# A mixture-of-experts kernel on one core: expert 0 computed in the small form too, so that small and large experts alternate from the start

## The chip, the core and the metric

The kernel runs on one core of a Trainium2 chip. The metric is device microseconds (us) of one execution; lower is better. A core has five instruction streams that run by themselves and meet at semaphores: TensorE (PE, matmuls; its weight loads are shown apart as PEld), VectorE (DVE), ScalarE (ACT), GpSimd (POOL) and SyncE (SP, which here issues nearly all DMAs). PE reads SBUF and writes PSUM, a small memory of eight banks. PE's clock has two levels, 1.2 and 2.4 GHz; the profile gives the granted share of the higher one.

## The reference, cut to what matters

Two layers over 256 tokens of width 1024. Each is a mixer (differential attention, pooling, a gated recurrence, one output projection), a layer norm, a feed-forward part and a layer norm. In layer 0 the feed-forward part is a dense SwiGLU; in layer 1 each token goes to the best 2 of 8 experts, and this is where the change lies:

```python
def _swiglu(x, w_gate, w_up, w_down):
    return (jax.nn.silu(x @ w_gate) * (x @ w_up)) @ w_down

def _moe_swiglu(x, w_router, w_gate, w_up, w_down):
    logits = (xt @ w_router).astype(jnp.float32)
    top_logit, top_e = lax.top_k(logits, TOP_K)          # 2 of 8
    gate = jax.nn.softmax(top_logit, axis=-1)
    ...                                                  # rows of each expert gathered
    ys = lax.map(expert_block, ...)                      # _swiglu(rows, w_gate[e], w_up[e], w_down[e])
    contrib = ys[dest] * gate.reshape(-1)[order][:, None]
    return jnp.zeros_like(xt).at[tok].add(contrib)
```

An expert's matrices are 1024 x 2816, 1024 x 2816 and 2816 x 1024 in float32, 34.6 MB together; all eight are read once, 276.8 MB of the 344.8 MB that the core reads from HBM.

## The kernel before

**Two forms of an expert.** A *large* expert has 128 places for tokens. Each 1 MB tile of its weights (`weight`, L102 to L117) is split into a high part (ACT, L112) and a rest (DVE, L114), and every product is three matmuls at one pass each: high x high, high x low, low x high (`up_part`, L941; `down_part`, L1014). Its stationary operands are the gathered tokens `xgh`, `xgl`, 128 columns wide. A *small* expert has 64 places. Its weights are used as they come, in float32, without a split (`small_up_part`, L960; `small_down_part`, L986): a matmul has 64 stationary columns (`xs`, `hs`), and two that stand side by side use the two column halves of the array. The profile shows each float32 matmul as two records.

**Which expert is which.** Position 0 of the order is always expert 0. The others are ranked by their number of tokens (`order_experts`, L900, on DVE: comparisons and sums over 8 x 8 tables), and `RANKS` says which rank stands at which position: 0, 5, 1, 6, 2, 7, 3, 4. Ranks 5 to 7 (the three with the fewest tokens) are small, the others, expert 0 among them, large. The numbers of the chosen experts are loaded into registers of SP (`weights_at`, L1091), which computes the weights' addresses from them.

**Groups.** `GROUPS` says which positions are gathered together (`gather`, L852): for each group, 32 matmuls pick the tokens' rows with a one-hot matrix `O` and leave them in PSUM; copies bring them to `xgh`, `xgl` (large) and `xs` (small). Before, groups are expert 0 alone, three times small with large, and the last large one alone.

**The step loop.** (L1100 and on) An expert is cut into chunks of its 2816 hidden columns: 512 (large) or 1024 (small). In each step the gate and up products of a chunk are issued, and the down products of the chunk before it. An expert's last chunk issues the next group's gather; an expert's result is spread back to the tokens by one-hot matmuls and added with the gate's factor (`combine`, `small_combine`). A scheduler orders each engine's instructions by a simulated timeline, within what dependences allow.

**Buffers.** Weight tiles go through a ring of 13 buffers of 1 MB (5 in `rawp`, 8 in `more`), used in turn. SP issues a tile's DMA when its buffer is free: in a large expert when ACT and DVE have split it, in a small one when PE has multiplied with it.

**Too many tokens.** `overflow` (L1149) runs a loop over all experts when any expert has more tokens than places. In the profiled execution it is skipped.

Of the kernel before, what the change touches and what calls it, by code (L numbers as in the profile page):

```python
# [8 lines left out]
F32 = mybir.dt.float32  # L9
F32R = mybir.dt.float32r  # L10
I32 = mybir.dt.int32
# [5 lines left out]
P = 128  # L17
T = 256
NT = T // P
D = 1024  # L20
KD = D // P
# [6 lines left out]
NE = 8  # L28
# [10 lines left out]
FILL = (6, 4, 5)  # L39


RANKS = (0, 5, 1, 6, 2, 7, 3, 4)
FIRST_SMALL = 5
SMALL = tuple(r >= FIRST_SMALL for r in RANKS)
GROUPS = ((0,), (1, 2), (3, 4), (5, 6), (7,))
HALF = 64
TINY, EDGE = 160, 480

# [7 lines left out]
def trunk(ctx, tc, x, w_in, w_out, col_params, row_params, block_params,  # L56
          ln1_g, ln1_b, ln2_g, ln2_b, ffn_w_gate, ffn_w_up, ffn_w_down,
          router_w, moe_w_gate, moe_w_up, moe_w_down, out):
    nc = tc.nc
    vec, act, gp, pe = nc.vector, nc.scalar, nc.gpsimd, nc.tensor  # L60
# [668 lines left out]
    place = R("place", [P, NT, NE])  # L729
# [84 lines left out]
    mo = moe.enter_context(tc.tile_pool(name="mo", bufs=1))  # L814
    acc = x_nat
    mot = moe.enter_context(tc.tile_pool(name="mot", bufs=1))
    M = lambda nm, shape, dt=F32, tag=None: (mo if tag else mot).tile(shape, dt, tag=tag or "m_" + nm, name="m_" + nm)
# [14 lines left out]
    def places(place_cols, small):  # L832

        O = const.tile([P, NT, 2, P], F32R, tag="O", name="O")
        for t in range(NT):
            for j, of_half in enumerate(small):
                last = vec.tensor_scalar(O[:, t, j, :], halves.rearrange("p a b -> p (a b)") if of_half else slots,
                                         place_cols[:, t, j:j + 1], None, op0=ALU.is_equal)
        return O[:, :, 0:len(small), :], last

    def turn_places(O):

        n = O.shape[2]
        OT = mo.tile([P, 2, NT, P], F32R, tag="OT", name="OT")
        tp = psC.tile([P, 2, NT, P], F32, tag="tp", name="tp")
        for j in range(n):
            for t in range(NT):
                pe.transpose(tp[:, j, t, :], O[:, t, j, :].bitcast(F32), ident)
        act.copy(OT[:, 0:n, :, :], tp[:, 0:n, :, :])
        return OT  # L850

    def gather(O, small, wide=False):  # L852

        n = len(small)
        xg = (mo.tile([P, KD, P], F32R, tag="xgh", name="xgh"), mo.tile([P, KD, P], F32R, tag="xgl", name="xgl"))
        xs = mo.tile([P, KD, HALF], F32, tag="xs", name="xs") if small[0] else None
        for k in range(0, KD, 2):
            for i in range(2):
                pool, tag = (psA, "gu") if wide else ((psD, "sg"), (psC, "tp"))[i]
                ps = pool.tile([P, 2, 2, P], F32, tag=tag, name="ps_g")  # L860
                for j in range(2):
                    for t in range(NT):
                        pe.matmul(ps[:, j, 0:n, :], xn[i][:, t, (k + j) * P:(k + j + 1) * P], O[:, t, :, :],
                                  start=(t == 0), stop=(t == NT - 1))
                (vec.tensor_copy if i and not wide else act.copy)(xg[i][:, k:k + 2, :], ps[:, :, n - 1, :])
                if xs is not None:
                    part_ = ps[:, :, 0, 0:HALF]
                    act.copy(xs[:, k:k + 2, :], part_) if i == 0 else vec.tensor_add(xs[:, k:k + 2, :], xs[:, k:k + 2, :], part_)
        return xg, xs
# [26 lines left out]
        vec.tensor_mul(gate, gate, den[:, :, None].to_broadcast([P, NT, NE]))  # L896

    small64 = M("small64", [P, NE])

    def order_experts():  # L900

        key = M("key", [P, NE])
        vec.tensor_copy(key, tokens)
        vec.memset(key[:, 0:1], float(2 * T))
        le = key[:, :, None].to_broadcast([P, NE, NE])
        lj = key[:, None, :].to_broadcast([P, NE, NE])
        c1 = M("c1", [P, NE, NE], tag="yh")
        c2 = M("c2", [P, NE, NE], tag="yl")
        rank = M("rank", [P, NE])
        vec.tensor_tensor(c1, lj, le, op=ALU.is_gt)  # L910
        vec.tensor_tensor(c2, lj, le, op=ALU.is_equal)
        vec.tensor_mul(c2, c2, lower)
        vec.tensor_add(c1, c1, c2)
        vec.reduce_sum(rank, c1, axis=AX.X)

        vec.tensor_tensor(c1, rank[:, None, :].to_broadcast([P, NE, NE]), ranks[:, :, None].to_broadcast([P, NE, NE]),
                          op=ALU.is_equal)
        at = M("at", [P, NE])
        vec.tensor_mul(c2, c1, numbers[:, None, :].to_broadcast([P, NE, NE]))
        vec.reduce_sum(at, c2, axis=AX.X)  # L920
        vec.tensor_copy(chosen, at)
        for src, name in ((place, "place_s"), (gate, "gate_s")):
            to = M(name, [P, NT, NE])
            for t in range(NT):
                vec.tensor_mul(c2, c1, src[:, t, None, :].to_broadcast([P, NE, NE]))
                vec.reduce_sum(to[:, t, :], c2, axis=AX.X)
            routed.append(to)

        vec.tensor_scalar(small64, rank, float(FIRST_SMALL), float(P - HALF), op0=ALU.is_ge, op1=ALU.mult)
        vec.tensor_add(at, tokens, small64)  # L930
        vec.tensor_reduce(key[:, 0:1], at, axis=AX.X, op=ALU.max)
        vec.tensor_copy(count, key[:, 0:1])

# [3 lines left out]
    def expert_weights(e):  # L937

        return [w[0][bass.ds(e, 1), :, :].rearrange("e a b -> (e a) b") for w in (moe_w_gate, moe_w_up, moe_w_down)]
# [57 lines left out]
    def glu(pg, pu, n):  # L997
        sg = mo.tile([P, FC], F32, tag="sg", name="sg")
        act.activation(sg[:, :n], pg[:, :n], AF.Silu)  # L999
        vec.tensor_mul(sg[:, :n], pu[:, :n], sg[:, :n])  # L1000
        return sg

    def turn(f, n, hh, last=False):

        nk = n // P
        tp = psC.tile([P, 4, P], F32, tag="tp", name="tp_h")
        for k in range(nk):
            pe.transpose(tp[:, k, :], hh[:, k * P:(k + 1) * P], ident)
        tags = ("xgh", "xgl") if last else ("hTh", "hTl")
        hT = [mo.tile([P, 2, 2, P], F32R, tag=tag, name="hT").rearrange("p a b c -> p (a b) c") for tag in tags]  # L1010
        split_to(hT[0][:, :nk, :], hT[1][:, :nk, :], tp[:, :nk, :])
        return hT

    def down_part(ws, py, f, n, hT):  # L1014

        nk = n // P
        for k0 in range(0, nk, 2):
            w = weight(rows(ws[2], f // P + k0, 2))
            for k in range(2):
                first, last = f + k0 + k == 0, f + (k0 + k + 1) * P == DFF  # L1020
                halves = [(py[nn], slice(nn * 512, (nn + 1) * 512)) for nn in range(2)]
                for i in range(2):
                    for ps, s in halves:
                        pe.matmul(ps, hT[i][:, k0 + k, :], w[k][0][:, s], start=(first and i == 0), stop=False)  # L1024
                for ps, s in halves:
                    pe.matmul(ps, hT[0][:, k0 + k, :], w[k][1][:, s], start=False, stop=last)  # L1026
# [14 lines left out]
    def y_banks():  # L1041
        return [psB.tile([P, 512], F32, tag="y", name="py") for n in range(2)]
# [103 lines left out]
                act.activation(acc[:, t, :], x_nat[:, t, :], AF.Copy, scale=ALPHA)  # L1146


    def overflow():  # L1149
        most = nc.values_load(count[0:1, 0:1], min_val=0, max_val=T + P - HALF)  # L1150
        with tc.If(most > P):
            rings[:] = [rawp] * RAW_BUFS
            hold[:] = [None]
            vec.tensor_add(place, place, small64[:, None, :].to_broadcast([P, NT, NE]))
            for _ in range(2):
                vec.tensor_scalar_add(slots, slots, float(P))
                with tc.For_i(0, NE, 1) as e:
                    pg_e = mot.tile([P, 2, NT, 2], F32, tag="pg_e", name="pg_e")
                    for j in range(2):
                        vec.tensor_copy(pg_e[:, 0, :, j:j + 1], place[:, :, bass.ds(e, 1)])  # L1160
                        vec.tensor_copy(pg_e[:, 1, :, j:j + 1], gate[:, :, bass.ds(e, 1)])
                    O, _ = places(pg_e[:, 0, :, :], (False,))
                    OT = turn_places(O)
                    xg, _ = gather(O, (False,))
                    ws = expert_weights(e)
                    py = y_banks()
                    for f, n in chunks:
                        down_part(ws, py, f, n, turn(f, n, glu(*up_part(ws, xg, f, n), n)))
                    combine(OT[:, 0, :, :], pg_e[:, 1, :, 0:1], py)
            for t in range(NT):  # L1170
                vec.reduce_sum(sums[:, t, :], acc[:, t, :].rearrange("p (a b) -> p a b", a=2), axis=AX.X)
            squares(sums)
# [45 lines left out]
```

## Time and profile before

| what | us |
|---|---|
| median of 3 runs (1137.21 to 1139.38) | 1137.24 |
| the profiled execution | 1140.82 |
| its span, first to last instruction | 1139.1 |
| PE busy in the span | 1100.1 |
| DVE busy in the span | 734.4 |
| ACT busy in the span | 590.7 |

The span is cut into pieces by the trace: up to about 414 us lie layer 0, the mixer of layer 1 and the routing, then the eight experts, and the last 17 us are the sums of the last expert, the layer norm and the output. PE's busy time has modelled ends, so a busy PE is not yet a PE at its peak. A row `x4` of a timeline stands for four instructions in a row.

### The profile page before, as it was taken

To read this page: it belongs to the slowest core of one execution; us is meant where nothing else is said; L and a number is where in the kernel's file an instruction comes from. 1 tells how busy PE (TensorE), PEld (TensorE's weight loads), DVE (VectorE), ACT (ScalarE), POOL (GpSimd) and SP (SyncE) were. 2 spreads that over 40 slices of the span, in tenths; PEclk is the share of its full clock that TensorE was granted. 3 is DMA by queue.
4 is the path that set the end of the run, shared out by engine and by line. 5 is a ranking of instruction groups with operands and counts; after the bars stand their busy time and mean duration, and the time that the engine had idled before them with its cause. 6 is when DMAs were issued, how large, how long until landed. Compare 5 with 4: busy or idle time off the path is not lost. (4 is left out here: it accounts for less than half of the span.)

```text
span 1139.1 us, 15821 instructions
## 1 busy us (share of the span) xinstructions
PE 1100.1 (97%) x6017; PEld 848.3 (74%) x6017; DVE 734.4 (64%) x938; ACT 590.7 (52%) x798; POOL 25.4 (2%) x64
## 2 busy tenths in 40 slices
PE   8989999999998999999999999999999999999995
PEld 8978999999897888874357883347883347888883
DVE  6777655455867669961148972048972049898986
ACT  5764544444466458750146751046751046777673
POOL 1001000000100100000000000000000000000000
PEclk9989999999998969999999999999999999999998
DMA  9732755565464849989999999999999999999931
GB/s 320 279 115 92 259 186 186 186 186 185 153 215 148 332 161 354 375 296 378 411 414 412 411 407 388 380 413 412 410 419 393 376 413 412 407 411 367 360 119 39
DMA packets 158660, 346.93 MB, mean 305 GB/s; under 512 B 8164, under 2 KB 59504, under 8 KB 158576
## 3 DMA queue, kind: packets, MB, share of 16 engines
q1 hardware_dynamic: 158400, 345.56, 81.1%
q8 instruction: 49, 0.80, 0.3%
q14 instruction: 35, 0.29, 0.1%
q10 hardware_dynamic: 144, 0.26, 0.1%
q0 software_dynamic: 32, 0.02, 0.0%
HBM read 344.77 MB, written 1.05 MB: 304 GB/s over the span
## 5 line engine op out<-in xcount | busy, mean ns | idle before, releaser
L114 DVE TENSOR_TENSOR lo<-raw,hi 128x1024 fp32r<-128x1024 f32 x446 | 525.4, 1219 | 151.8 <-ACT hi L112 149.2
L112 ACT CAST hi<-raw 128x1024 fp32r<-128x1024 f32 x446 | 444.6, 1050 | 139.8 <-issue 54.1
L144 PE MATMUL mm<-xh,hi 128*128 128x256 f32 x512 | 147.2, 288 | 0.0
L146 PE MATMUL mm<-xl,hi 128*128 128x256 f32 x512 | 146.2, 286 | 0.0
L145 PE MATMUL mm<-xh,lo 128*128 128x256 f32 x512 | 146.1, 286 | 0.0
L1024 PE MATMUL py<-hi,hT 128*128 128x512 f32 x432 | 117.4, 392 | 0.0
L144 PEld LDWEIGHTS mm<-xh,hi 128*128 128x128 f32 x512 | 99.6, 195 | 0.9
L145 PEld LDWEIGHTS mm<-xh,lo 128*128 128x128 f32 x512 | 99.5, 194 | 0.4
L146 PEld LDWEIGHTS mm<-xl,hi 128*128 128x128 f32 x512 | 99.4, 194 | 0.0
L1024 PEld LDWEIGHTS py<-hi,hT 128*128 128x128 f32 x432 | 80.3, 188 | 17.6 <-issue 0.8
L955 PE MATMUL pg<-hi,xgh 128*128 128x512 f32 (+1 forms) x240 | 90.3, 381 | 3.2 <-ACT hi L112 3.2
L955 PE MATMUL pg<-hi,xgl 128*128 128x512 f32 (+1 forms) x240 | 89.1, 376 | 0.0
L955 PE MATMUL pu<-hi,xgh 128*128 128x512 f32 (+1 forms) x240 | 88.4, 374 | 0.0
L955 PE MATMUL pu<-hi,xgl 128*128 128x512 f32 (+1 forms) x240 | 88.0, 372 | 0.0
L1000 DVE TENSOR_TENSOR sg<-pu,sg 128x512 f32<-128x512 f32 (+2 forms) x39 | 25.2, 645 | 88.1 <-PE pu L972 65.1
L957 PE MATMUL pg<-lo,xgh 128*128 128x512 f32 (+1 forms) x240 | 69.9, 379 | 0.5 <-DVE lo L114 0.4
L1026 PE MATMUL py<-lo,hT 128*128 128x512 f32 x216 | 69.0, 401 | 0.0
L972 PE MATMUL pg<-raw,xs 128*64 128x512 f32 (+1 forms) x288 | 68.9, 563 | 0.0
L972 PE MATMUL pu<-raw,xs 128*64 128x512 f32 (+1 forms) x288 | 68.8, 561 | 0.0
L957 PE MATMUL pu<-lo,xgh 128*128 128x512 f32 (+1 forms) x240 | 68.7, 374 | 0.0
L999 ACT ACTIVATE sg<-pg 128x512 f32<-128x512 f32 (+2 forms) x39 | 21.9, 561 | 88.5 <-PE pg L957 49.5
L994 PE MATMUL py<-raw,hs 128*64 128x512 f32 x264 | 60.4, 599 | 0.7 <-ACT hs L983 0.7
(296 smaller groups left out, 1416.5 us busy)
## 6 DMA issues: line engine op xcount, KB each, us to landing
raw<-in_moe_w_down_dram SPq DMA_DIRECT2D x87, 1024.0 KB, 10.5
raw<-in_moe_w_gate_dram SPq DMA_DIRECT2D x79, 1024.0 KB, 11.4
raw<-in_moe_w_up_dram SPq DMA_DIRECT2D x79, 1024.0 KB, 11.3
raw<-in_w_in_dram SPq DMA_DIRECT2D x17, 1024.0 KB, 5.6
raw<-in_ffn_w_gate_dram SPq DMA_DIRECT2D x11, 1024.0 KB, 5.2
raw<-in_ffn_w_up_dram SPq DMA_DIRECT2D x11, 1024.0 KB, 5.2
raw<-in_ffn_w_down_dram SPq DMA_DIRECT2D x11, 1024.0 KB, 5.0
raw<-in_moe_w_gate_dram SPq DMA_DIRECT2D x12, 768.0 KB, 7.6
```

Of the source, the lines that this page charges most:

```text
L112: act.copy(hi, raw[:, s, :])
L114: last_lo[:] = [vec.tensor_sub(lo, raw[:, s, :], hi.bitcast(F32))]
L144: pe.matmul(ps, lh, rh, start=first, stop=False)
L145: pe.matmul(ps, ll, rh, start=False, stop=False)
L146: return pe.matmul(ps, lh, rl, start=False, stop=last)
L955: pe.matmul(ps[:, :n], xg[i][:, k0 + k, :], w[k][0], start=(k0 + k + i == 0), stop=False)
L957: pe.matmul(ps[:, :n], xg[0][:, k0 + k, :], w[k][1], start=False, stop=(k0 + k == KD - 1))
L972: pe.matmul(ps[h * HALF:(h + 1) * HALF, :n], xs[:, k0 + k, :], raw[:, k, h * n:(h + 1) * n], start=(k0 + k == 0), stop=(k0 + k == KD - 1))
L994: pe.matmul(py[nn * HALF:(nn + 1) * HALF, :], hs[:, k % nk, k // nk, :], raw[:, k - k0, nn * 512:(nn + 1) * 512], start=(f + k == 0), stop ...
L1000: vec.tensor_mul(sg[:, :n], pu[:, :n], sg[:, :n])
L1024: pe.matmul(ps, hT[i][:, k0 + k, :], w[k][0][:, s], start=(first and i == 0), stop=False)
L1026: pe.matmul(ps, hT[0][:, k0 + k, :], w[k][1][:, s], start=False, stop=last)
```

## The change

Expert 0 gets the small form, with 64 places. The positions become expert 0 (small), rank 1 (large), rank 5 (small), rank 2 (large), rank 6 (small), rank 3 (large), rank 7 (small), rank 4 (large). Expert 0 and the large one behind it are gathered each by itself; the rest in pairs small with large. `gather` makes no large copies where the group has no large expert. `ends` keeps each expert's token number (with 64 added for the small ones), and the loop of `overflow` looks at each expert's before it does the work, which moved into `more_places`.

```diff
-RANKS = (0, 5, 1, 6, 2, 7, 3, 4)
+RANKS = (0, 1, 5, 2, 6, 3, 7, 4)
 FIRST_SMALL = 5
-SMALL = tuple(r >= FIRST_SMALL for r in RANKS)
-GROUPS = ((0,), (1, 2), (3, 4), (5, 6), (7,))
+SMALL = tuple(r == 0 or r >= FIRST_SMALL for r in RANKS)
+GROUPS = ((0,), (1,), (2, 3), (4, 5), (6, 7))
...
-        xg = (mo.tile([P, KD, P], F32R, tag="xgh", name="xgh"), mo.tile([P, KD, P], F32R, tag="xgl", name="xgl"))
+        xg = None if small[-1] else [mo.tile([P, KD, P], F32R, tag=tag, name="xg") for tag in ("xgh", "xgl")]
...
-                (vec.tensor_copy if i and not wide else act.copy)(xg[i][:, k:k + 2, :], ps[:, :, n - 1, :])
+                if xg is not None:
+                    (vec.tensor_copy if i and not wide else act.copy)(xg[i][:, k:k + 2, :], ps[:, :, n - 1, :])
...
+    ends = M("ends", [P, NE], I32)
...
+        vec.memset(small64[:, 0:1], float(P - HALF))
         vec.tensor_add(at, tokens, small64)
+        vec.tensor_copy(ends, at)
...
-            for _ in range(2):
+            for r in range(2):
                 vec.tensor_scalar_add(slots, slots, float(P))
                 with tc.For_i(0, NE, 1) as e:
...
+                    end = nc.values_load(ends[0:1, bass.ds(e, 1)], min_val=0, max_val=T + P - HALF)
+                    with tc.If(end > (r + 1) * P):
+                        more_places(e)
```

Lines behind the changed ones move by a few numbers: L955, L957 become L959, L961 (large up products), L972 becomes L976 (small up), L994 becomes L998 (small down), L969 and L991 (their DMAs) L973 and L995, L1094 becomes L1098.

PE at the start of the experts, before: behind the gather (`ps_g`) of expert 0 stand large matmuls, three for each piece of weight (`hi`, `lo`).

```order
L792 MATMUL pc<-r_sel,ones 128x8
L863 MATMUL ps_g<-O,xn 128x128 x32
L955 MATMUL pg<-hi,xgh 128x512
L955 MATMUL pg<-hi,xgl 128x512
L955 MATMUL pg<-hi,xgh 128x512
L955 MATMUL pg<-hi,xgl 128x512
L957 MATMUL pg<-lo,xgh 128x512 x2
```

The same place of the changed kernel: small matmuls on the unsplit weights (`raw`, `xs`), and the transposes of the first chunk's product (`tp_h`) behind 56 of them, 24 of these from the second chunk; then the down products (`py`), more up products, and the gather of the next expert in pieces of 8.

```order
L863 MATMUL ps_g<-O,xn 128x128 x32
L976 MATMUL pg<-raw,xs 64x512 x8
...
L985 MATMUL tp_h<-ident,sg 128x128 x4
L976 MATMUL pg<-raw,xs 64x512 x4
...
L998 MATMUL py<-raw,hs 64x512 x16
...
L863 MATMUL ps_g<-O,xn 128x128 x8
L998 MATMUL py<-raw,hs 64x512 x12
L863 MATMUL ps_g<-O,xn 128x128 x8
L998 MATMUL py<-raw,hs 64x512 x4
L959 MATMUL pg<-hi,xg 128x512 x4
```

So the first expert's large matmuls are gone from there, and large ones begin behind three chunks of small ones.

SP before, at the loads of the expert numbers into registers (`m_chosen`; `count` is the highest token number): they stand behind the 21st weight tile, with one more tile among them.

```order
L107 DMA raw<-in_moe_w_up_dram 128x4x512
L107 DMA raw<-in_moe_w_down_dram 128x2x1024
L1094 TENSOR_LOAD m_chosen
...
L107 DMA raw<-in_moe_w_down_dram 128x2x1024
L1094 TENSOR_LOAD m_chosen
...
L1150 TENSOR_LOAD count
L1150 ISA x2
L107 DMA raw<-in_moe_w_gate_dram 128x4x512
```

SP in the changed kernel: the eight loads (seven of `m_chosen`, one of `count`) stand together, behind the 13th weight tile and ahead of the 14th.

```order
L973 DMA raw<-in_moe_w_up_dram 128x2x1024
L973 DMA raw<-in_moe_w_gate_dram 128x2x1024
L1098 TENSOR_LOAD m_chosen
...
L1168 TENSOR_LOAD count
L1168 ISA x2
L973 DMA raw<-in_moe_w_up_dram 128x2x1024
L973 DMA raw<-in_moe_w_gate_dram 128x2x1024
```

The loads have moved ahead by eight tiles. On DVE the sums that they read from are no longer mixed with splits (L114) but follow each other, with the adds of the gather between.

## Rows read from the trace of the kernel before

**Rows 1.** The page: PE, and the bytes moved in 40 slices.
```profile
PE 1100.1 (97%) x6017; PEld 848.3 (74%) x6017; DVE 734.4 (64%) x938; ACT 590.7 (52%) x798; POOL 25.4 (2%) x64
GB/s 320 279 115 92 259 186 186 186 186 185 153 215 148 332 161 354 375 296 378 411 414 412 411 407 388 380 413 412 410 419 393 376 413 412 407 411 367 360 119 39
```
**Rows 2.** Windows, one for each stage: length, busy time (count), clock, DMA, GB/s.
```profile
core 0: us, PE busy (x) PEld busy (x) DVE busy (x) ACT busy (x) POOL busy (x), PEclk, DMA share, GB/s
414.20:508.70 94.50, 94.50 (x448) 79.00 (x447) 81.74 (x104) 70.52 (x78) 0.00 (x0) 0.97 0.93 342
508.70:679.70 171.00, 169.17 (x788) 105.20 (x787) 94.17 (x102) 75.69 (x96) 0.00 (x0) 1.00 1.01 398
679.70:851.00 171.30, 166.29 (x786) 103.75 (x785) 96.45 (x104) 77.04 (x96) 0.00 (x0) 1.00 1.02 402
851.00:1022.30 171.30, 166.10 (x788) 103.93 (x787) 96.86 (x102) 79.45 (x97) 0.00 (x0) 1.00 1.03 402
1022.30:1122.10 99.80, 99.80 (x482) 83.54 (x481) 88.68 (x89) 71.09 (x84) 0.00 (x0) 1.00 0.69 254
```
**Rows 3.** Timeline of PE at four places: start, us, what.
```profile
414.21 0.73 PE L955 MATMUL pg<-hi,xgh 128*128 128x512 f32 x1
...
821.42 0.39 PE L955 MATMUL pg<-hi,xgh 128*128 128x512 f32 x1
...
1090.93 0.39 PE L955 MATMUL pg<-hi,xgh 128*128 128x512 f32 x1
...
1121.69 0.39 PE L146 MATMUL py<-lo,hT 128*128 128x512 f32 x1
```
**Rows 4.** Waits of PE in 679.7 to 851: total us, times, longest.
```profile
PE tp_h L981 <- DVE sg L1000: 2.5, 3, 0.9
PE pg L955 <- ACT hi L112: 1.6, 1, 1.6
PE ps_c L1074 <- ACT yh L130: 0.7, 1, 0.7
PE ps_c L1074 <- DVE yl L130: 0.2, 1, 0.2
```
**Rows 5.** Windows at the start of the experts.
```profile
414.00:416.00 2.00, 2.00 (x6) 1.64 (x7) 0.00 (x0) 0.37 (x1) 0.00 (x0) 0.50 1.00 403
416.00:418.00 2.00, 2.00 (x6) 1.58 (x5) 0.66 (x1) 1.04 (x1) 0.00 (x0) 0.50 1.04 395
418.00:420.00 2.00, 2.00 (x7) 1.58 (x7) 0.75 (x4) 1.05 (x1) 0.00 (x0) 0.67 0.36 141
```
**Rows 6.** Timeline of PE: combine, small up products, gather, down products.
```profile
705.35 0.50 PE L1060 MATMUL ps_c<-yh,OT 128*128 128x512 f32 x1
...
706.02 1.94 PE L972 MATMUL pg<-raw,xs 128*64 128x512 f32 x8
...
848.62 1.11 PE L863 MATMUL ps_g<-O,xn 128*128 128x256 f32 x8
849.57 0.63 PE L1026 MATMUL py<-lo,hT 128*128 128x512 f32 x2
850.04 1.08 PE L1024 MATMUL py<-hi,hT 128*128 128x512 f32 x4
```
**Rows 7.** Timeline of SP: the 13th weight tile, and the issues around the register loads.
```profile
383.54 1.24 SPq L107 DMA_DIRECT2D raw<-in_moe_w_gate_dram  x1
...
434.03 2.96 SPq L107 DMA_DIRECT2D raw<-in_moe_w_down_dram  x2
439.95 0.37 SPq L107 DMA_DIRECT2D raw<-in_moe_w_gate_dram  x1
```
**Rows 8.** Timeline of DVE: token sums, the first splits, the highest count.
```profile
407.53 0.17 DVE L794 COPY r_tokens<-pc 128x8 f32<-128x8 f32 x1 [0.26 <-PE pc L792]
...
407.89 5.79 DVE L114 TENSOR_TENSOR lo<-raw,hi 128x1024 fp32r<-128x1024 f32 x5
...
438.55 0.14 DVE L932 CAST count<-m_key 128x1 int32<-128x1 f32 x1
```
**Rows 9.** Windows: mostly a large expert, and a small one alone.
```profile
545.00:690.00 145.00, 143.17 (x678) 95.55 (x679) 92.79 (x100) 72.79 (x90) 0.00 (x0) 1.00 1.03 408
690.00:720.00 30.00, 28.27 (x125) 10.42 (x122) 8.82 (x14) 5.41 (x8) 0.00 (x0) 1.00 1.01 395
```

More of the change, by code (lines that the diff above doesn't have):

```diff
@@ L1146, in trunk, with more_places @@
                 act.activation(acc[:, t, :], x_nat[:, t, :], AF.Copy, scale=ALPHA)
+    def more_places(e):
+        pg_e = mot.tile([P, 2, NT, 2], F32, tag="pg_e", name="pg_e")
+        for j in range(2):
+            vec.tensor_copy(pg_e[:, 0, :, j:j + 1], place[:, :, bass.ds(e, 1)])
+            vec.tensor_copy(pg_e[:, 1, :, j:j + 1], gate[:, :, bass.ds(e, 1)])
+        O, _ = places(pg_e[:, 0, :, :], (False,))
+        OT = turn_places(O)
+        xg, _ = gather(O, (False,))
+        ws = expert_weights(e)
+        py = y_banks()
+        for f, n in chunks:
+            down_part(ws, py, f, n, turn(f, n, glu(*up_part(ws, xg, f, n), n)))
+        combine(OT[:, 0, :, :], pg_e[:, 1, :, 0:1], py)
     def overflow():
@@ L1154, in overflow @@
             vec.tensor_add(place, place, small64[:, None, :].to_broadcast([P, NT, NE]))
-            for _ in range(2):
+            for r in range(2):
                 vec.tensor_scalar_add(slots, slots, float(P))
                 with tc.For_i(0, NE, 1) as e:
[L1158 to L1169, printed above, removed]
+                    end = nc.values_load(ends[0:1, bass.ds(e, 1)], min_val=0, max_val=T + P - HALF)
+                    with tc.If(end > (r + 1) * P):
+                        more_places(e)
             for t in range(NT):
```

## The prediction

> **What bounds the kernel now.** I read the page first, then the windows by stage, then the PE timeline and the waits of one stage. The last layer's experts run from 414.21 us (first expert matmul) to 1121.69 us (last down matmul starts) [rows 3]: 707.5 us of a span of 1139.1. In the order of the program that is large (expert 0), then small-large three times, then large. By the windows [rows 2] the first large one takes 94.5 us, a small-large pair 171.0, 171.3 and 171.3 us, the last large one 99.8 us. In every one of them PE is busy nearly all the time (94.5 of 94.5, 166 to 169 of 171, 99.8 of 99.8), while the weights come in at 398 to 402 GB/s in a pair, but only 342 in the first large one and 254 in the last. So in the two large ones at the ends PE is the bound alone and the transfers wait for free buffers; in a pair PE is the bound with the transfers close behind: the page's slices with the highest rate show 411 to 419 GB/s [rows 1]. In a pair PE waits 5.0 us in all, and no entry of that list is a DMA [rows 4]: 2.5 us are transposes waiting for the gated product, 1.6 us a large expert's first matmul waiting for a split.
>
> **The change part by part.**
>
> *Expert 0 small.* The program becomes four pairs small-large. The later places keep their PE order: the order of the last three pairs is that of the old three pairs but for a few gather matmuls. So I put the new stage together from old pieces, measured from a pair's first matmul to the next pair's first:
> - Two middle pairs: mean of 171.0, 171.3, 171.3 is 171.2 each, 342.4 us [rows 2].
> - Last pair, up to its last down matmul: the second old pair starts at 679.7 and its fifth big chunk starts on PE at 821.42, 141.7 us later. The old last large expert needed from the same point (1090.93) to its last down matmul (1121.69) 30.8 us, and no other work lay between. Together 172.5 us. One early group of four gather matmuls for a following expert goes: 8 take 848.62 to 849.57, so 0.5 us [rows 3, 6]. 172.0 us.
> - First pair: 171.3, less what an earlier large expert leaves over in a pair: four combine steps of 0.67 us (705.35 to 706.02), 2.7, and 14 trailing down matmuls at 0.235 (849.57 to 850.04 for two), 3.3. Plus 20 gather matmuls more, since expert 0 and the next large one are now gathered separately (52 against 32 in a pair): 20 times 0.12, 2.4 us. Plus the slow clock: the granted clock is 0.50 of full speed (the 1.2 GHz level) until 418 and 0.67 on average to 420 [rows 5], which costs 4 x 0.5 + 2 x 0.33 = 2.7 us, and should cost the same under small matmuls. That is 170.4. Less waits: in the new PE order each of expert 0's transposes stands at least 24 matmuls behind the chunk it needs, so the 2.5 us that transposes wait in a pair should go. The other 2.5 us may go or stay. I take 170.4 - 2.5 = 167.9; the ends are 165.4 (all 5.0 us of [rows 4] gone) and 175 (none gone, and another 5 us of new waits, as much as a pair has now).
>
> Sum: 167.9 + 342.4 + 172.0 = 682.3 us against 707.5, **25.2 us less**. A check from the other side: a pair less a large expert, 171.3 - 99.8 = 71.5 us, is what a small one costs, so swapping one should give 28.3 us; the 3 us of difference are mostly the first expert's 94.5 us, of which less can be saved.
>
> *What stands ahead of the stage.* The 32 gather matmuls stay. The copies after them change from ACT alone to ACT copy and DVE add in turn; the early splits of expert 0's weights on ACT and DVE go. That no longer competes with routing, but I find nothing on the path that waited for it: 0, with bounds from -2 us to +3 us (about one split, 1.2 us [rows 8], more or less at each of two places).
>
> *The eight register loads on SP.* They now stand ahead of the 14th weight transfer and behind the routing sums on DVE. Behind them on SP wait all further weights. In the old trace the 13th transfer is issued at 383.54 and 13 buffers then hold back the next; the new kernel has the same 13. The eight loads lay between two old issues, 434.03 and 439.95, with one other transfer between: at most 5.5 us for all, the wait for the last count included [rows 7]. That count was ready at 438.55, 31.0 us after the token sums at 407.53, but 18 splits of some 1.2 us each (five of them are the row of 5.79 us) and the waits for their first halves were in that stretch [rows 8]; without them I estimate 4 to 6 us, so 412 to 414, and the 14th transfer at 417 to 420. PE frees the first buffer only at about 418 (from 414.2 one 1 MB tile of small matmuls, 1.94 us [rows 6], at half clock, for each of gate and up), so the loads cost nothing or 2 us of transfer time. The cover is the 13 tiles: they last PE some 13 x 1.94 + 2.7 = 28 us, to 442.
>
> *Are the transfers in time?* Eight experts have 8 x 34.6 MB (three matrices of 1024 x 2816 in float32), 276.8 MB, 13.6 of them there at the start. The other 263.2 MB from 420 on at the 402 GB/s of a pair end at 420 + 655 = 1075; the last down matmul is due at 414.2 + 682.3 = 1096.5. At the 395 GB/s of a small stretch [rows 9] they end at 1086. So PE stays last, with 10 to 20 us in hand.
>
> The Trainium skill, DMA: Bandwidth & Descriptors, section Bandwidth (Where 436 GB/s comes from), speaks against this: it says that transfers from HBM to SBUF are bound by HBM at about 358 GB/s per core. By that rule the 263.2 MB would take 735 us, end at 1155, and the change would gain nothing. The trace does not agree: it shows 398 to 402 GB/s over 171 us [rows 2], so the sum goes by the trace and the rule gets no chance.
>
> *The rest.* The new `ends` copy and the memset are two small DVE operations on 128x8; the routing's own of that kind last 0.14 to 0.17 us [rows 8], between others that nothing waits for before 418: nothing. The test in the loop stands in a branch that is skipped unless an expert has more than its places, as before. Routing the reference's own inputs (its default seed) gives expert 0 59 tokens of 256 (59, 76, 44, 73, 71, 41, 48, 100 for the eight), under the 64 places. The tail of the span behind the last down matmul, 17.4 us, stays.
>
> **The forecast.** The profiled execution took 1140.82 us (its span 1139.1), the median is 1137.24. The sum is made on the profiled one, 0.3% above the median and so the same kernel at the same pace; I subtract it from the median: 1137.2 - 25.2 = **1112 us**. Its own range: the first pair's ends give 1109.5 to 1119; the middle and last pairs go with the transfers' limit of 412 GB/s below (69.2 MB in 168 us, 3 us less each, 9 in all: 1100) and 1 us each above: 1101 to 1122.
>
> **The rivals.**
> 1. *The transfers become the bound.* In the new program half of the time is small experts, where the rate shows 395 instead of 408 GB/s [rows 9], and the register loads may hold the 14th transfer. If it starts at 442 (PE out of tiles; the count as late as the old 438.55 plus loads) and the rate is 395, the weights end at 442 + 666 = 1108, and the last chunk behind them takes about 10 us: 1118 for the last down matmul, 3.5 us less than before: 1133. With only one of the two it is 1098 to 1107: 1113 to 1123. For it: 2 to 3% of headroom. Against it: no wait of PE for a DMA in a pair. Decides from 22 us of lateness on. Price taken: 1123.
> 2. *The clock stays low under small matmuls (slower).* In the old kernel the clock rises at 418 to 420 under large matmuls; every small stretch starts at full clock. Should expert 0's stretch run at the 1.2 GHz level, its stretch, at most the 71.5 us worked out above and dense (PE busy 28.27 of 30 us [rows 9]), doubles: 1112 + 71.5 = 1184. It decides from 50 us at the lower level on, where the loss of half of each us eats the 25 us. Against it: small stretches hold 1.00 in all windows [rows 2, 9], and the gather ahead is as before. The Trainium skill, TensorE: Matmul & The Clock Gate, part 1, has the lower level as the default that matmul work lifts and idleness brings back; it gives no reason for rival 2 as long as PE is fed, and the trace agrees in so far as no small stretch falls.
> 3. *Expert 0 has over 64 tokens where it is timed (the change does not do what it says).* Then the skipped branch runs: one large expert without prefetch, at least 94.5 us [rows 2], plus 16 turns of a loop that no row shows: over 1112 + 95 = 1207. Decides at 65 tokens; 59 is counted, so only other inputs could do it.
>
> **How the numbers follow.** Forecast 0.82, rival 1 0.11, rival 2 0.03, rival 3 0.03, none of these 0.01. The predicted time is the forecast's, 1112. Its range 1101 to 1122 is narrowed by 2 us below, where all pairs would have to run at the transfers' limit, and 1 us is added above for rival 1's price: 1103 to 1123. A difference within 0.2% (2.3 us) can't be told from none. Faster holds the forecast and nearly all of rival 1: 0.92; same 0.02, from rival 1's worst case; slower 0.06, rivals 2 and 3.
>
> **What would show it.** Right: first small matmul at 414 (+-3), second pair at 582, third at 753, fourth at 924, last down matmul near 1096; 400 GB/s and more from 425 on; the clock at 1.00 from 420. The slices at the end would no longer show PE working for 30 us without transfers. Wrong: PE idle before small matmuls with a DMA as releaser (rival 1); a clock of 0.50 beyond 425 (rival 2); expert instructions behind 1110 us with a large expert's matmuls (rival 3); pairs longer than 173 us, which would say that a pair's time depends on what the pair before it left in the buffers.

## The result, and the profile after

The changed kernel takes 1111.78 us (median of 4 runs, 1109.48 to 1113.36), beside 1138.27 us for the one before in the same comparison: ratio 0.9762, 95% interval 0.9741 to 0.9782, 26.5 us less. The forecast was 1112 us. One run in this document, of the version with the transposes held back below, had a mean granted clock of 0.554 and took 1760.04 us; it is left out of that version's median. The profiled execution took 1113.36 us (span 1111.6), 27.5 us less than the profiled one of before (1140.82).

The page of the changed kernel, PE and the bytes moved in 40 slices of 27.8 us:

```profile
PE 1067.3 (96%) x5866; PEld 788.6 (71%) x5867; DVE 654.5 (59%) x869; ACT 518.6 (47%) x722; POOL 24.8 (2%) x65
GB/s 311 291 112 113 265 168 181 190 184 189 127 263 141 261 117 350 414 413 413 409 419 419 414 414 412 406 419 398 386 414 411 409 420 371 374 412 412 411 208 41
```

Beside [rows 1] PE is busy 32.8 us less. The transfers run at 371 to 420 GB/s in all slices from the 17th to the 38th; before, the first large expert held three slices at 296 to 375. In the next to last slice 208 GB/s are left: at 412 that is at most 14 us after its start at 1056, so the weights are there by about 1070, and PE goes on to 1094.

Timeline of PE, changed kernel (start, us, what, idle time and releaser): the gather, the first small matmuls, the first large ones, the starts of the later pairs and the last down matmul.

```profile
408.41 7.06 PE L863 MATMUL ps_g<-O,xn 128*128 128x128 f32 x32 [1.01 <-DVE m_key L906]
415.40 5.34 PE L976 MATMUL pg<-raw,xs 128*64 128x512 f32 x16
...
424.01 1.88 PE L976 MATMUL pg<-raw,xs 128*64 128x512 f32 x8
425.72 1.88 PE L976 MATMUL pu<-raw,xs 128*64 128x512 f32 x8
...
473.13 1.19 PE L959 MATMUL pg<-hi,xg 128*128 128x512 f32 x4
...
577.38 1.94 PE L976 MATMUL pg<-raw,xs 128*64 128x512 f32 x8
579.25 0.74 PE L1030 MATMUL py<-lo,hT 128*128 128x512 f32 x2
...
585.27 0.44 PE L1012 MATMUL tp_h<-ident,sg 128*128 128x128 f32 x2
585.64 1.94 PE L976 MATMUL pu<-raw,xs 128*64 128x512 f32 x8
...
748.81 1.94 PE L976 MATMUL pg<-raw,xs 128*64 128x512 f32 x8
...
921.73 1.94 PE L976 MATMUL pg<-raw,xs 128*64 128x512 f32 x8
...
1093.86 0.39 PE L146 MATMUL py<-lo,hT 128*128 128x512 f32 x1
```

From the first expert matmul to the last down matmul it is 678.5 us for 707.5 [rows 3], 29.0 less. The stage begins 1.2 us later, and 0.3 us are added behind it. The four pairs as windows (columns as in [rows 2]):

```profile
415.40:577.40 162.00, 162.00 (x784) 102.80 (x783) 90.21 (x98) 75.76 (x95) 0.00 (x0) 0.99 1.00 399
577.40:748.80 171.40, 166.20 (x786) 103.81 (x785) 96.39 (x104) 77.18 (x96) 0.00 (x0) 1.00 1.04 414
748.80:921.70 172.90, 167.88 (x786) 104.90 (x785) 96.47 (x104) 77.07 (x96) 0.00 (x0) 0.99 1.03 406
921.70:1094.20 172.50, 167.30 (x783) 104.43 (x783) 97.07 (x100) 78.43 (x94) 0.00 (x0) 1.00 0.88 342
```

The first pair is the odd one: 162.0 us, with PE busy in all of it. In each later pair PE waits 5.0 to 5.2 us. All waits of PE from 415 to 1094 (total us, times, longest); none of them lies in the first pair, and none is for a DMA:

```profile
PE tp_h L985 <- DVE sg L1004: 7.4, 9, 0.9
PE pg L959 <- ACT hi L112: 4.7, 3, 1.6
PE ps_c L1078 <- ACT yh L130: 2.1, 3, 0.7
PE ps_c L1078 <- DVE yl L130: 0.7, 3, 0.2
PE pg L961 <- DVE lo L114: 0.4, 2, 0.2
```

### The profile page after: what moved, and what is told of

It is laid out like the page before. It is cut to its first block, busy times and chain, and to the rows that moved or that the text cites. A ratio compares the mean times of both kernels' runs of the same rounds, so it can differ in the third digit from the quotient of the medians.

```text
span 1111.6 us, 15280 instructions
## 1 busy us (share of the span) xinstructions
PE 1067.3 (96%) x5866; PEld 788.6 (71%) x5867; DVE 654.5 (59%) x869; ACT 518.6 (47%) x722; POOL 24.8 (2%) x65
## 5 line engine op out<-in xcount | busy, mean ns | idle before, releaser
L114 DVE TENSOR_TENSOR lo<-raw,hi 128x1024 fp32r<-128x1024 f32 x380 | 446.8, 1221 | 143.8 <-ACT hi L112 143.2
L112 ACT CAST hi<-raw 128x1024 fp32r<-128x1024 f32 x380 | 375.9, 1049 | 124.5 <-issue 54.3
L959 PE MATMUL pg<-hi,xg 128*128 128x512 f32 (+1 forms) x384 | 97.0, 378 | 4.7 <-ACT hi L112 4.7
L959 PE MATMUL pu<-hi,xg 128*128 128x512 f32 (+1 forms) x384 | 95.0, 373 | 0.0
L1028 PE MATMUL py<-hi,hT 128*128 128x512 f32 x344 | 92.9, 392 | 0.0
L976 PE MATMUL pg<-raw,xs 128*64 128x512 f32 (+1 forms) x384 | 86.2, 571 | 0.0
L976 PE MATMUL pu<-raw,xs 128*64 128x512 f32 (+1 forms) x384 | 84.3, 561 | 0.0
L959 PEld LDWEIGHTS pg<-hi,xg 128*128 128x128 f32 x384 | 68.4, 190 | 22.0 <-ACT hi L112 8.1
L998 PE MATMUL py<-raw,hs 128*64 128x512 f32 x352 | 79.9, 598 | 0.0
L959 PEld LDWEIGHTS pu<-hi,xg 128*128 128x128 f32 x384 | 68.3, 189 | 13.5 <-issue 0.7
L976 PEld LDWEIGHTS pg<-raw,xs 128*64 128x64 f32 x384 | 26.3, 139 | 44.8 <-issue 41.7
L976 PEld LDWEIGHTS pu<-raw,xs 128*64 128x64 f32 x384 | 26.2, 137 | 43.9 <-issue 41.6
L961 PE MATMUL pg<-lo,xg 128*128 128x512 f32 (+1 forms) x192 | 56.6, 383 | 0.6 <-DVE lo L114 0.4
```

The source lines that it names most:

```text
L112: act.copy(hi, raw[:, s, :])
L114: last_lo[:] = [vec.tensor_sub(lo, raw[:, s, :], hi.bitcast(F32))]
L959: pe.matmul(ps[:, :n], xg[i][:, k0 + k, :], w[k][0], start=(k0 + k + i == 0), stop=False)
L961: pe.matmul(ps[:, :n], xg[0][:, k0 + k, :], w[k][1], start=False, stop=(k0 + k == KD - 1))
L976: pe.matmul(ps[h * HALF:(h + 1) * HALF, :n], xs[:, k0 + k, :], raw[:, k, h * n:(h + 1) * n], start=(k0 + k == 0), stop=(k0 + k == KD - 1))
L998: pe.matmul(py[nn * HALF:(nn + 1) * HALF, :], hs[:, k % nk, k // nk, :], raw[:, k - k0, nn * 512:(nn + 1) * 512], start=(f + k == 0), stop ...
```

## The experiments

My theory: PE bounds the stage, and the gain is the PE work that a small expert does not have; the turns of small and large keep the transfers just in time. Rivals: the gain is from the other edits; from the order alone; or the transfers bind already. All ratios are to the kernel before, run on the same chip beside it.

**The rest of the change alone.**

```diff
-RANKS = (0, 1, 5, 2, 6, 3, 7, 4)
+RANKS = (0, 5, 1, 6, 2, 7, 3, 4)
-SMALL = tuple(r == 0 or r >= FIRST_SMALL for r in RANKS)
-GROUPS = ((0,), (1,), (2, 3), (4, 5), (6, 7))
+SMALL = tuple(r >= FIRST_SMALL for r in RANKS)
+GROUPS = ((0,), (1, 2), (3, 4), (5, 6), (7,))
...
-        vec.memset(small64[:, 0:1], float(P - HALF))
```

> Only the rest of the change is left in: expert 0 is large again and stands where it stood (ranks, forms and groups of before), while the ends of each expert, the body of the rare branch as a function of its own and the gather without the tiles nobody reads stay. My theory: the gain is PE work that the small form of expert 0 leaves out, so nothing is left of it: 1137 to 1140 us, as before. Rival (the other edits bring the gain): about 1112.

Measured: 1137.78 us, ratio 1.0001 (0.9982 to 1.0020). The other edits are worth nothing that shows (the interval is 2 us to either side); that rival is out.

**Expert 0 small, in the old order.**

```diff
-RANKS = (0, 1, 5, 2, 6, 3, 7, 4)
-GROUPS = ((0,), (1,), (2, 3), (4, 5), (6, 7))
+RANKS = (0, 5, 1, 6, 2, 7, 3, 4)
+GROUPS = ((0,), (1, 2), (3, 4), (5, 6), (7,))
```

> Expert 0 is small, but the other experts keep the order of before, so that two small experts come first and two large ones last (S S L S L S L L). If only the sum of PE's work counts: 1112, as after. My theory: also the transfers must keep up in each stretch. The two small ones take 57.7 and some 66 us on PE, their 66 tiles of 1 MB, 14 of them there at 420, land at 2.55 us each (412 GB/s) by 553 to 556, against 541 on PE, and what is lost there is not won back by a large expert: 1126 (1119 to 1134). Rival (the gain is from turns, small and large, alone): 1137 or more.

Measured: 1117.44 us, ratio 0.9822 (0.9798 to 0.9845), 5.7 us over the changed kernel and clear of its interval. So the small form gives about 20 of the 26 us by itself and the turns the rest. The timeline of PE in the second small expert shows how the rest is lost:

```profile
524.42 1.51 PE L976 MATMUL pu<-raw,xs 128*64 128x384 f32 x8 [0.40 <-DMA raw<-in_moe_w_up_dram]
...
537.25 1.51 PE L976 MATMUL pu<-raw,xs 128*64 128x384 f32 x8 [1.84 <-DMA raw<-in_moe_w_up_dram]
...
547.10 1.94 PE L998 MATMUL py<-raw,hs 128*64 128x512 f32 x8 [0.52 <-DMA raw<-in_moe_w_down_dram]
550.74 1.21 PE L959 MATMUL pg<-hi,xg 128*128 128x512 f32 x4 [1.70 <-ACT hi L112]
```

From 520 us on nearly every tile is waited for: 6.1 us in eleven waits of PE for a DMA, an entry that PE's lists of the kernel before and of the changed one do not have. Windows of the same kernel, the starved stretch and the one behind it:

```profile
512.00:550.70 38.70, 29.43 (x141) 8.73 (x137) 1.25 (x2) 2.63 (x6) 0.00 (x0) 1.00 1.03 416
550.70:556.00 5.30, 5.22 (x15) 3.88 (x16) 4.82 (x5) 4.11 (x5) 0.00 (x0) 0.68 1.05 416
```

PE is busy 29.43 of 38.7 us while the transfers run at 416 GB/s, and the granted clock is 0.68 in the 5.3 us behind it, a loss of 1.7 us. The stage takes 686.7 us, 8.2 more than in the changed kernel. The direction was as expected, the size was below my range (1117.4 for 1119 to 1134): I had charged PE with all tiles of both small experts, but three tiles of the second one's down products (24 of 88 records) stand behind the first large matmul at 550.74, so they may land later. At 2.55 us a tile that is 7.6 us of the 12 to 15 that I had counted; no run tests this account.

**Less PE work.**

```diff
-                            pe.matmul(ps[:, :n], xg[i][:, k0 + k, :], w[k][0], start=(k0 + k + i == 0), stop=False)
-                    for k in ks:
-                        pe.matmul(ps[:, :n], xg[0][:, k0 + k, :], w[k][1], start=False, stop=(k0 + k == KD - 1))
+                            pe.matmul(ps[:, :n], xg[i][:, k0 + k, :], w[k][0], start=(k0 + k + i == 0), stop=(k0 + k == KD - 1 and i == 1))
```

> After, without the third product (high part of x by low part of the weights) in the large experts' up part; splits and transfers stay. A chunk then has 32 matmuls for 48, 3.7 us of 11.1 less, 20.3 us for an expert, 81 for four. PE alone: 1031. My theory: PE binds by a small margin, and the transfers are next: 250 tiles after 420 at 2.55 us end at 1058, some 4 us to the last matmul, 18 us of tail: 1085 (1076 to 1095). Rival (transfers bind in after already): 1112, no change.

Measured: 1084.01 us, ratio 0.9532 (0.9511 to 0.9552): 27.8 us less than the changed kernel for some 81 us less of matmuls (an estimate, 384 of them at the pace of 0.23 us and half of that for narrow ones). Bytes moved in 40 slices of its span, from its page:

```profile
GB/s 328 286 117 110 244 191 195 175 179 191 148 241 156 175 252 206 418 411 413 412 413 420 418 415 413 410 413 420 417 416 412 412 410 420 418 415 413 413 403 89
```

Its stage as one window:

```profile
414.20:1065.20 651.00, 605.06 (x2750) 336.71 (x2749) 376.46 (x406) 309.65 (x381) 0.00 (x0) 1.00 1.02 407
```

With less to do PE is busy 605 of 651 us, and the transfers hardly pause: 410 to 420 GB/s in the 22 slices from the 17th on, then 403 and 89. So PE does bind in the changed kernel, with a second bound some 28 us below it. That the transfers bind already is out. The Trainium skill, HBM Reference, section Specifications (TRN2), gives 358 GB/s as a core's share and says that a core streaming alone measures about 425; the trace, 407 GB/s over 651 us on one core, lies nearer the second figure.

**More transfers.**

```diff
     def small_up_part(ws, xs, f, n, between=None):
+
+        nc.sync.dma_start(raw_tile([P, 2, D]), rows(ws[2], f // P, 2))
```

> After with 12 more weight tiles of 1 MB, one at the head of each of the 12 small chunks, which nothing reads: 30.6 us of transfers at 412 GB/s. If the transfers bind: 1142. If PE binds everywhere with much to spare: 1112. My theory: the spare is small where small experts run: the first loses some 8 us, each later one 4 to 5, while a large expert hides its part: 1130 (1118 to 1135).

Measured: 1121.34 us, ratio 0.9869 (0.9848 to 0.9891): 9.6 us over the changed kernel for 30 us more of transfers. Windows of its four small stretches:

```profile
414.40:474.10 59.70, 59.70 (x300) 22.89 (x299) 5.12 (x10) 7.33 (x14) 0.00 (x0) 0.97 0.95 378
...
579.10:645.90 66.80, 62.29 (x298) 23.09 (x297) 10.64 (x21) 8.91 (x16) 0.00 (x0) 1.00 1.03 417
...
750.60:819.80 69.20, 63.06 (x299) 22.81 (x297) 10.69 (x20) 8.95 (x16) 0.00 (x0) 1.00 1.03 418
...
924.50:995.20 70.70, 63.54 (x300) 22.55 (x298) 9.87 (x17) 8.99 (x16) 0.00 (x0) 1.00 1.03 418
```

The second stretch of the changed kernel, for comparison:

```profile
577.40:645.40 68.00, 63.96 (x309) 24.36 (x308) 11.08 (x21) 8.91 (x16) 0.00 (x0) 1.00 1.03 417
```

In the changed kernel the four take 57.7, 68.0, 68.0 and 68.0 us. The lengths can't be compared as they are, since gather matmuls have moved between the stretches: the first grows by 2.0 us with PE busy in all of it (16 more gather matmuls stand in it now). PE's idle time can: 0, 4.5, 6.1 and 7.2 us, where the changed kernel has 0, 4.0, 4.0 and 4.0. It looks as if the lead of the 13 buffers is used up by degrees, where I had charged every small expert with its own three tiles. PE's waits for a DMA are 4.0 us in all. The stage takes 684.9 us, 6.4 more than in the profile above and 8.4 more than in a second profile of the changed kernel (676.5, below). The result lies in the lower part of my range, 9 us under my forecast of 1130.

**The waits of the later pairs.** The transposes of h (`tp_h`) are issued ahead of the last tiles of the next chunk in the code, but the scheduler put them straight behind the chunk they need. The next kernel pins them where the code has them; `mm` is the last matmul that stands ahead of `between()`.

```diff
+        mm = None
         for k0 in range(0, KD, 2):
             if k0 + 2 == KD and between is not None:
-                between()
+                with after(mm):
+                    between()
...
-                        pe.matmul(ps[h * HALF:(h + 1) * HALF, :n], xs[:, k0 + k, :], raw[:, k, h * n:(h + 1) * n],
+                        mm = pe.matmul(ps[h * HALF:(h + 1) * HALF, :n], xs[:, k0 + k, :], raw[:, k, h * n:(h + 1) * n],
```

(and the same in `up_part`). The second edit gives the transposed h two buffers:

```diff
-        hs = mo.tile([P, 4, 2, HALF], F32, tag="hs", name="hs")
+        hs = mo.tile([P, 4, 2, HALF], F32, tag="hs", bufs=2, name="hs")
```

The changed kernel itself ran beside them; its trace is called the second profile below:

> The changed kernel itself, unaltered, beside the three that follow: 1112 (1109 to 1114) by every theory.

The transposes held back:

> After, with the four transposes of a chunk of h held back behind the matmuls of the next chunk that stand ahead of them in the code, so that silu and product are done when their turn comes; the small expert's copy of them then stands behind the first splits of the large one. In after, PE waits 7.4 us in nine places for that product and 4.7 us in three for the first split. My theory (PE binds, and 24 us lie between the last landing and the last matmul): both go, less something that the transfers take back in small stretches: 1102 (1099 to 1107). Rival (the transfers are as near as the two small experts in a row showed): the waits change their name, 1110 to 1113.

Two buffers:

> After, with two buffers for the transposed h of a small expert, so that its copy, and the splits queued behind it on ScalarE, need not wait for the last matmuls that read the old one. My theory: only the 4.7 us (three waits for the first split, 1.6 each) go: 1107.5 (1105 to 1110). Rival (the split comes late since its tile lands late): 1112.

Both:

> The transposes held back and the two buffers together. My theory: holding back alone already frees the splits, so the second buffer adds next to nothing: 1102 (1098 to 1107). Rival: the gains add, 12 us and more, 1100 or less.

Measured: the changed kernel again 1112.39 us, ratio 0.9766 (0.9748 to 0.9784); transposes held back **1097.94 us** (1098.73 with the run of 1760 us counted, which makes the 13.7 us of the last expectation below), 0.9648 (0.9627 to 0.9669); two buffers 1107.36 us, 0.9715 (0.9697 to 0.9732); both 1099.91 us, 0.9659 (0.9640 to 0.9678). Both together are not told apart from holding back alone. The version with the transposes held back beats both kernels of this case, the changed one by some 14 us (14.4 by the medians, 13.4 by the ratios). PE's waits from the gather on:

```profile
PE py L1034 <- DVE lo L114: 2.6, 3, 0.9
PE ps_c L1082 <- ACT yh L130: 2.1, 3, 0.7
PE ps_g L863 <- DVE m_key L906: 1.0, 1, 1.0
PE ps_c L1082 <- DVE yl L130: 0.7, 3, 0.2
PE pg L963 <- DVE lo L114: 0.4, 2, 0.2
```

Both entries aimed at are gone (12.1 us), and 2.6 us of new ones came. Its pairs:

```profile
411.20:572.70 161.50, 161.50 (x784) 102.73 (x783) 90.42 (x98) 75.88 (x95) 0.00 (x0) 0.99 1.01 400
572.70:740.80 168.10, 166.13 (x788) 103.90 (x787) 96.49 (x104) 77.48 (x96) 0.00 (x0) 1.00 1.04 414
740.80:908.70 167.90, 166.12 (x788) 103.62 (x787) 96.51 (x104) 77.71 (x96) 0.00 (x0) 1.00 1.04 415
908.70:1077.70 169.00, 167.03 (x783) 104.42 (x783) 97.15 (x100) 78.62 (x94) 0.00 (x0) 1.00 0.91 361
```

The stage is 10.3 us shorter than in the second profile (666.2 against 676.5 us). That much the edit is shown to give. The rest of the 14 us lies ahead of the stage, which begins at 411.2 for 414.3 in these two profiles; the last section says what was different there, and that the edit causes it is not shown. The rival, that waits would only change their name, is out. Two buffers gave 5.0 us for the 4.7 expected, but not quite in the way expected. The 4.7 us for the first split become 1.2 more for its rest, and the first pair is 3.8 us longer (165.5 for 161.7): 1.2 us are that wait, 0.9 are matmuls at the lower clock, since the stage begins 1.3 us earlier while the clock rises as late as before, and some 1 us more goes to down products that the gather now cuts into smaller pieces. So the stage is only 2.2 us shorter, and the other part of the gain is not accounted for.

**The same edit in the kernel before.** The diff is the one above.

> The kernel before with the transposes held back as in the run that did this to the changed kernel (there 13.7 us). My theory: the three later small experts have the same waits in both kernels (7.4 us for the product, 4.7 for the first split), so the two edits are independent: 1139 less 11 to 14, 1126 (1123 to 1129), and the change keeps its 25 to 28 us on top. Rival (the waits stood on the path only since the change had brought the transfers forward): 1134 to 1140.

Measured: 1130.26 us, ratio 0.9936 (0.9914 to 0.9958), 8.1 us less, outside my range and not the rival either. The size was wrong for a reason that the list of waits of before, over all its experts, shows:

```profile
PE tp_h L981 <- DVE sg L1000: 4.9, 6, 0.9
PE pg L955 <- ACT hi L112: 3.2, 2, 1.6
```

I had taken the waits of three small experts; only two of the three have them, 8.1 us together. In both kernels it is the first small expert that has none. Both entries are gone in the trace of this run, and a new one has come:

```profile
PE py L1030 <- DVE lo L114: 1.7, 2, 0.9
```

So 6.4 us of waits went, the stage is 7.8 us shorter (699.7 for 707.5), and that the medians differ by just 8.1 is chance. It also means that the two edits are not independent: with the transposes held back in both kernels the change is worth some 32 us (1130.26 against 1097.94), for 26.5 without; the stages differ by 33.5 us, for 29.0. One reason is that the changed kernel has three small experts with such waits and the one before two.

## Why the prediction was right

*PE is the bound, transfers close behind.* Shown from both sides: with some 81 us less of matmuls the time falls by 27.8 us until the transfers bind; with 30 us more of transfers it rises by 9.6. The prediction's 10 to 20 us in hand were some 24: the transfers end by about 1070 and not at 1075 to 1086, since they ran at 406 and 414 GB/s in the two middle pairs for the assumed 395 to 402.

*The middle and last pairs:* 171.4 and 172.9 us for 171.2, and 172.1 to the last down matmul for 172.0. The 1.7 us too much in one of them are a spell of lower clock, told below; in the second profile of the same kernel that pair takes 171.3.

*The first pair* is the term that was mis-sized: 162.0 us for 167.9, below the 165.4 that I had given as its end (161.7 in the second profile). Of the steps in it: all 5.0 us of the waits went, not 2.5, which makes 2.5 us. The slow clock cost 1.7 us for 2.7, since the stage began later and the clock was 0.79 in 418 to 420 for the assumed 0.67:

```profile
414.00:416.00 2.00, 2.00 (x9) 1.57 (x10) 0.57 (x3) 1.33 (x2) 0.00 (x0) 0.50 0.00 0
416.00:418.00 2.00, 2.00 (x6) 0.47 (x4) 0.00 (x0) 0.22 (x1) 0.00 (x0) 0.50 0.00 0
418.00:420.00 2.00, 2.00 (x10) 0.66 (x8) 0.00 (x0) 0.00 (x0) 0.00 (x0) 0.79 0.00 0
420.00:422.00 2.00, 2.00 (x12) 0.70 (x10) 0.00 (x0) 0.00 (x0) 0.00 (x0) 1.00 0.89 244
```

And I took the pace of a small tile from a stretch where other matmuls stand between. There a tile of eight records takes 1.87 us to the next instruction (577.38 to 579.25), while without anything between one starts every 1.71 us (424.01 to 425.72): about 0.15 us for a tile. In the timeline the small matmuls of the second pair stand in 15 unbroken runs and those of the first pair in 8. Added up from each start to the next, without waits and without the slow clock's 1.7 us, they take 59.3 us in the second pair and 57.8 in the first: 1.5 us. Two smaller steps were off too. The 20 gather matmuls more cost 2.0 us for 2.4. And an earlier large expert leaves two transposes in a pair, 0.4 us (585.27 to 585.64), which my list had left out. Together 2.5, 1.0, 1.5, 0.4 and 0.4 make 5.8 of the 5.9 us. The check by "a pair less a large expert", 28.3 us, which I had set aside, came nearer to the 29.0 of the stage than the sum's 25.2; I had explained the 3 us between the two away.

*The start* was put at 0, with +3 as its bound: the stage begins 1.2 us later, 0.1 us in the second profile. In both PE's gather waits 1.01 us for DVE, where a copy of the token sums now goes ahead of the one-hot matrix. Since the start moves by more than that between profiles (last section), how much of the 1.2 us this wait costs is not shown. The wait is charged to the clearing of `m_key`, which runs beside the end of the matrix:

```profile
407.64 0.17 DVE L905 COPY m_key<-r_tokens 128x8 f32<-128x8 f32 x1
407.81 0.52 DVE L837 TENSOR_SCALAR O<-m_halves,r_place 128x128 fp32r<-128x128 f32 x2
...
408.35 0.06 DVE L906 MEMSET m_key<- 128x1 f32 x1
...
412.37 0.15 DVE L936 CAST count<-m_key 128x1 int32<-128x1 f32 x1
```

*The register loads* went as predicted: the count is there at 412.37 (412 to 414), and the 14th transfer is issued at 419.07 (417 to 420), released by PE and not by the loads.

*The rivals.* Transfers as the bound: no wait of PE for a DMA in the changed kernel. The clock under small matmuls: 1.00 from 420. Pairs over 173 us: none, though the 172.9 with the spell of lower clock is near it. The branch for too many tokens: nothing of it behind the last expert.

So the hit is partly luck. The medians differ by 26.5 us for the forecast's 25.2, because a first pair that was 5.9 us too dear stands against 1.2 us at the start, 2.1 in the later pairs, 0.3 at the end, and 1 us by which the two medians lie nearer than the two profiles. And the time itself, 1111.78 for 1112, is hit closer than the difference because the kernel before took 1138.27 us in the comparison, 1 us more than the 1137.24 that I subtracted from.

## What to carry to other kernels

When a stage is bound by one engine with another close behind, work out both budgets stretch by stage: here the cheaper form alone gave 20 us, and the order that lets cheap and dear experts take turns gave 6 more. Piece a new program together from measured pieces, but take a piece's pace from neighbours like those it will have, and ask of each wait whether the place it stands in exists in the new order. When two ways of reckoning differ, as 25.2 and 28.3 did here, find out why before setting one aside. Waits of under 1 us that recur at each chunk are worth a look in the order of instructions: pinning the transposes made the stage 10.3 us shorter for a few lines.

## What the hardware showed beside that

- The granted clock fell for a short spell in the changed kernel, at a place where PE had waited for the first split of a large expert (windows of three us):

```profile
815.00:818.00 3.00, 1.42 (x6) 0.67 (x4) 1.22 (x2) 2.67 (x4) 0.00 (x0) 1.00 1.02 421
818.00:821.00 3.00, 2.94 (x7) 2.36 (x8) 3.00 (x4) 3.00 (x4) 0.00 (x0) 0.53 1.02 411
821.00:824.00 3.00, 3.00 (x13) 2.37 (x13) 3.00 (x4) 2.38 (x3) 0.00 (x0) 0.90 1.05 410
```

  0.53 is the 1.2 GHz level for nearly all of the 3 us. The same wait at 645.4 and at 989.7, with PE busy 1.42 of 3 us there too, was followed by 1.00, and the second profile has no such spell, so it does not come every time. It cost some 1.6 us.
- In the routing ahead of the experts the clock falls to 0.50 at a time that differs between profiles: between 396 and 400 in the three profiles of the two kernels, at 406 to 407 in the version with the transposes held back, whose stage began 3 us earlier. Over all profiles the stage begins between 407.0 and 415.4 us. No run here tells what sets the moment.
